# Matmuls whose result nobody reads, placed at six points of a two-block transformer kernel

## The chip, the cores and the metric

The kernel runs on one core of one Trainium2 chip. The metric is the device time of one execution in microseconds (us). Engines are named as the profile names them: PE is TensorE (PEld its weight loads), DVE is VectorE, ACT is ScalarE, POOL is GpSimd, SP is SyncE, which issues most transfers. [...]

## The reference, cut to what matters

512 tokens of width 1024 go through two blocks, all in float32. The first block has a layer of gated linear attention and a layer of dilated attention over three groups, whose outputs are weighted by a softmax over the groups' log-sum-exps. The second block has a layer of latent and grouped attention over 512 tokens and 256 context tokens, a mixture of 32 experts (each token goes to 2), a layer of neighbourhood attention, and a second mixture. Norms stand between layers.

```
def first_block(...):
    for i in range(DEPTH):                  # 0: gla_mixer, 1: dilated_mixer
        h = rmsnorm(x, norm_w[i])
        ...
        branch = jnp.concatenate([mix, mem_o], axis=-1) * jax.nn.silu(gate)
        x = x + branch @ w_out[i]
    return rmsnorm(x, final_norm_w)

def dilated_mixer(h, w_in):
    ...
    wts = jax.nn.softmax(jnp.stack(lses, axis=0), axis=0)
    o = jnp.einsum('gbth,gbthd->bthd', wts, jnp.stack(outs, axis=0).astype(jnp.float32))

def second_block(...):
    for l in range(DEPTH):                  # 0: mixer_ab, 1: mixer_na
        h_l = modulate(x_lat, norm_mix[l], sh1, sc1)
        ...
        x_lat = x_lat + g1 * o_l
        h_l = modulate(x_lat, norm_ffn[l], sh2, sc2)
        y = hier_moe(tokens, moe_w_rg[l], ..., moe_w_gate[l], moe_w_up[l], moe_w_down[l])
        x_lat = x_lat + g2 * y...

def hier_moe(h, ...):                       # for each block of 128 tokens of one expert e:
    return (jax.nn.silu(xb @ w_gate[e]) * (xb @ w_up[e])) @ w_down[e]
```

## The kernel before, in words

Nearly all products are three fp32r products in place of one f32 product (`mm3`, L259 to L261): both factors are cut into a high and a low part, and high x high, high x low and low x high are added up in PSUM. Weights are loaded by SP in chunks (`pump`, L182) into slots called `wraw`; ACT writes the high part `whi` (L208), DVE the low part `wlo` (L211). A slot takes the next chunk once its low part is cut. `K.ready` is the queue of cut chunks.

Each stage is written as generators that yield costs, and `weave` runs them against one another, so the program's text order is interleaved by these costs. A scheduler then sets the order of instructions on every engine from its own model; each engine works through its row in that order.

The six places that matter here:

- **The norms between layers** (`norm_T`, L367). Four rows of 128 tokens, `K.tok` (`xres` in the profile), are scaled by ACT and DVE into `y` (L377, L379); then for k = 0..7 four 128x128 transposes (L386) fill one PSUM tile `ps_t`, and ACT and DVE write its high and low part (`dhh`, `dhl` ahead of the dilated layer, L390 and L391; through `nt`, L395, elsewhere). Ahead of the dilated layer and the ab layer this follows the last output projection, whose products go through L259 to L261 and are added to `xres` at L826.
- **The sums of w_ada** run beside the dilated layer: SP loads w_ada, DVE adds scaled rows into `acc` (L1393, L1395), and a product with a vector of ones (L1400) adds up the partitions. They hold DVE when a transfer is late.
- **The dilated layer's last softmax** (`Dil.joint` for t = 2). PE transposes the statistics `stT` (L1327), ACT and DVE work out the weights `jw`, PE transposes these (L1345), ACT copies them to `c6` (`c` in the profile), DVE writes the low part (L1347), and six products with a selection matrix spread them (L1352); DVE multiplies the groups' outputs (L1353). `values` (L1307) and the projection of the next part (L259 to L261 on `b`) go on around it.
- **The two expert stages** (`experts`, L2070). A table is made on DVE and PE (`table`; its last products are L2019, its results `idx`, `blk`). `overflow` is a loop of `blk` rounds (L2045 loads the count, L2046 is the loop), none in this data. Then `xg[0]`, the first expert's 128 tokens, is gathered by an indirect DMA on POOL (L2181), transposed on PE (`transposed`, L2192) into `ps_x`, copied into high and low (`xth`, `xtl`, L139 and L140), and multiplied by the gate and up weights into `ps_h`.

## Time and profile before

| | |
|---|---|
| time, median of 3 runs | 3178.2 us (3174.72 to 3180.22) |
| the profiled execution | 3179.87 us, span 3178.1 us |
| mean granted clock of PE | 0.958 |
| busy in the span: DVE, ACT, POOL | 71%, 56%, 18% |
| the chain that ended last, by engine | PE 80%, DVE 8%, ACT 4%, DMA 3%, issue 2% |
| instructions of PE | 17454 matmuls, 17454 weight loads |

Times in the profile are counted from the start of the span. A row of a timeline gives start, duration, engine, line, operation and tiles, the count, and in brackets how long the engine was idle before it and what ended that. Products of PE overlap, so the distance from one start to the next is the price of one, not its duration. A step of the chain has the part of the duration that lies on the chain. An f32 product appears as two records.

### The profile page before, as it was taken

To read this page: it belongs to the slowest core of one execution; us is meant where nothing else is said; L and a number is where in the kernel's file an instruction comes from. 1 tells how busy PE (TensorE), PEld (TensorE's weight loads), DVE (VectorE), ACT (ScalarE), POOL (GpSimd) and SP (SyncE) were. 2 spreads that over 40 slices of the span, in tenths; PEclk is the share of its full clock that TensorE was granted. 3 is DMA by queue.
4 is the path that set the end of the run, shared out by engine and by line. 5 is a ranking of instruction groups with operands and counts; after the bars stand their busy time and mean duration, and the time that the engine had idled before them with its cause. 6 is when DMAs were issued, how large, how long until landed. Compare 5 with 4: busy or idle time off the path is not lost.

```text
span 3178.1 us, 46855 instructions
## 1 busy us (share of the span) xinstructions
PE 2932.0 (92%) x17454; PEld 2455.8 (77%) x17454; DVE 2270.2 (71%) x3743; ACT 1793.7 (56%) x2971; POOL 567.2 (18%) x869
## 2 busy tenths in 40 slices
PE   7989899999889889996999999969998789999997
PEld 6858688888779777786888888858886778888885
DVE  4776656765555566657998899875445678988888
ACT  4543534343352466533887788854334368878885
POOL 2110143523232211032111111020001211111110
PEclk9989999999889899996999999989999889999998
DMA  6334333433431200034999999954334389999996
GB/s 209 126 113 139 140 125 115 148 132 133 153 122 29 76 28 1 1 116 148 362 374 374 344 360 367 365 171 141 100 100 142 140 292 370 351 331 347 353 366 203
DMA packets 146090, 636.32 MB, mean 200 GB/s; under 512 B 30787, under 2 KB 37283, under 8 KB 86850
## 3 DMA queue, kind: packets, MB, share of 16 engines
q1 hardware_dynamic: 104034, 568.56, 49.3%
q0 software_dynamic: 29664, 50.29, 5.0%
q10 hardware_dynamic: 12160, 14.43, 1.9%
q8 instruction: 139, 2.28, 0.3%
q14 instruction: 93, 0.76, 0.1%
HBM read 615.13 MB, written 48.58 MB: 209 GB/s over the span
## 4 chain that ended last, share of the span: by engine, by line
PE 80%; DVE 8%; ACT 4%; DMA 3%; issue 2%; POOL 1%; ACTq 0%; DVEq 0%; SPq 0%; POOLq 0%
PE ps_p L259 10%; PE ps_p L261 9%; PE ps_p L260 9%; PE ps_h L260 8%; PE ps_h L259 7%; PE ps_h L261 7%; PE ps_y L260 4%; PE ps_y L261 4%; PE ps_y L259 4%; PE ps_x L2192 2%; PE ps_o L574 2%; PE ps_t L562 2%; DVE wlo L211 2%; PE ps_o L470 1%; PE ps_t L490 1%
## 5 line engine op out<-in xcount | busy, mean ns | idle before, releaser
L211 DVE TENSOR_TENSOR wlo<-wraw,whi 128x1024 fp32r<-128x1024 f32 (+1 forms) x936 | 1104.7, 1221 | 243.4 <-ACT whi L208 238.9
L208 ACT ACTIVATE whi<-wraw 128x1024 fp32r<-128x1024 f32 (+1 forms) x938 | 936.2, 1050 | 185.8 <-PE ps_p L260 53.8
L260 PE MATMUL ps_h<-wlo,xth 128*128 128x512 f32 x1024 | 415.6, 406 | 1.3 <-DVE wlo L211 1.1
L259 PE MATMUL ps_h<-whi,xth 128*128 128x512 f32 x1024 | 409.1, 399 | 2.9 <-ACT xth L139 2.9
L261 PE MATMUL ps_h<-whi,xtl 128*128 128x512 f32 x1024 | 404.9, 395 | 0.0
L259 PE MATMUL ps_p<-whi,dhh 128*128 128x256 f32 (+3 forms) x828 | 248.6, 301 | 9.6 <-ACT qa L1540 5.7
L260 PE MATMUL ps_p<-wlo,dhh 128*128 128x256 f32 (+3 forms) x828 | 240.4, 291 | 0.0
L261 PE MATMUL ps_p<-whi,dhl 128*128 128x256 f32 (+3 forms) x828 | 239.7, 291 | 0.0
L259 PEld LDWEIGHTS ps_h<-whi,xth 128*128 128x128 f32 x1024 | 193.9, 189 | 47.9 <-ACT xth L139 4.0
L260 PEld LDWEIGHTS ps_h<-wlo,xth 128*128 128x128 f32 x1024 | 193.9, 189 | 47.7 <-DVE wlo L211 7.4
L261 PEld LDWEIGHTS ps_h<-whi,xtl 128*128 128x128 f32 x1024 | 193.5, 189 | 40.0
L259 PE MATMUL ps_y<-whi,hth 128*128 128x512 f32 x512 | 204.8, 400 | 5.8 <-DVE xg L2124 2.9
L1395 DVE SCALAR_TENSOR_TENSOR acc<-wraw,cs,acc 128x512 f32<-128x512 f32 x280 | 203.1, 758 | 9.2 <-DMA wraw<-in_w_ada_dram 7.5
L260 PE MATMUL ps_y<-wlo,hth 128*128 128x512 f32 x512 | 202.5, 395 | 0.2
L261 PE MATMUL ps_y<-whi,htl 128*128 128x512 f32 x512 | 201.9, 394 | 0.0
L2181 POOL DMA_INDIRECT xg<-hbuf,idx x64 | 85.3, 1333 | 547.2 <-PE ps_x L2192 494.5
L259 PEld LDWEIGHTS ps_p<-whi,dhh 128*128 128x128 f32 x828 | 157.7, 191 | 24.7 <-ACT qa L1540 5.9
L260 PEld LDWEIGHTS ps_p<-wlo,dhh 128*128 128x128 f32 x828 | 158.0, 191 | 1.3
L261 PEld LDWEIGHTS ps_p<-whi,dhl 128*128 128x128 f32 x828 | 157.7, 191 | 1.3
L2258 POOL DMA_INDIRECT ybuf<-y,idx x62 | 66.1, 1067 | 465.4 <-ACT y L2254 451.4
L139 ACT ACTIVATE xth<-ps_x 128x512 fp32r<-128x512 f32 x128 | 75.4, 589 | 76.7 <-PE ps_h L260 40.9
L259 PEld LDWEIGHTS ps_y<-whi,hth 128*128 128x128 f32 x512 | 96.3, 188 | 27.7 <-ACT whi L208 3.3
(788 smaller groups left out, 6766.1 us busy)
## 6 DMA issues: line engine op xcount, KB each, us to landing
wraw<-in_moe_w_gate_dram SPq DMA_DIRECT2D x128, 1024.0 KB
wraw<-in_moe_w_up_dram SPq DMA_DIRECT2D x128, 1024.0 KB
wraw<-in_moe_w_down_dram SPq DMA_DIRECT2D x128, 1024.0 KB
wraw<-in_w_ada_dram SPq DMA_DIRECT2D x48, 1024.0 KB
wraw<-in_db_w_dram SPq DMA_DIRECT2D x27, 1024.0 KB
wraw<-in_w_out_dram SPq DMA_DIRECT2D x8, 1024.0 KB
wraw<-in_na_qk_dram SPq DMA_DIRECT2D x8, 1024.0 KB
ntab<-in_na_tab_dram SPq DMA_DIRECT2D x16, 384.0 KB
```

What stands on the lines that cost most here:

```text
L139: nc.scalar.activation(hi, src, AF.Copy)
L208: self.nc.scalar.activation(h, x, AF.Copy)
L211: (self.cut_eng or self.nc.vector).tensor_tensor(l, x, h.bitcast(F32), op=OP.subtract)
L259: mm(out, ah, bh, start=first, stop=False)
L260: mm(out, ah, bl, start=False, stop=False)
L261: mm(out, al, bh, start=False, stop=last)
L562: nc.tensor.transpose(ps[:, b:b + 128], u.P[:, u.at[h, i], cols[m]:cols[m] + 128], K.ident)
L574: nc.tensor.matmul(po[64 * h:64 * h + 64, c:c + m], u.V(kt, h), pts[n][:, o_ + h * m:o_ + (h + 1) * m], start=(a == 0), stop=(a == last), ...
L1395: nc.vector.scalar_tensor_tensor(acc[s], x, w, acc[s], op0=OP.mult, op1=OP.add)
L2181: self.K.nc.gpsimd.indirect_dma_start(out=xg, out_offset=None, in_=self.hbuf, in_offset=bass.IndirectOffsetOnAxis(ap=gi, axis=0), bounds_c ...
L2192: nc.tensor.transpose(px[:, j * 128:(j + 1) * 128], xv[:, j, :], K.ident)
L2258: self.K.nc.gpsimd.indirect_dma_start(out=self.ybuf, out_offset=bass.IndirectOffsetOnAxis(ap=si, axis=0), in_=y, in_offset=None, bounds_ch ...
```

## The change

A helper `busy` issues n matmuls into a PSUM tile that is written again, from the start, by what follows; nobody reads what they write. It is called at these places:

- `norm_T` with `alone=True`, at three norms (ahead of the dilated, the ab and the neighbourhood layer): 7 f32 products, 128x128 by 128x512, ahead of the first four transposes, and 1 ahead of the four of each k = 1..7.
- `Dil.joint` at t = 2: 7 f32 products on `stT` (68 partitions, 512 columns) behind the transposes of `stT`, and 3 fp32r products (6 partitions, 512 columns) behind the copy of `c6`.
- `experts`: 24 fp32r products, 128x128 by 128x512, on the high part of the first cut weights, in the text behind the gathers and ahead of `transposed(xg[0])`. Both mixtures have it.

```diff
--- before.py
+++ after.py
@@ -260,6 +260,12 @@
         mm(out, ah, bl, start=False, stop=False)
         mm(out, al, bh, start=False, stop=last)
 
+    def busy(self, ps, a, b, n):
+        for _ in range(n):
+            self.nc.tensor.matmul(ps[:, :b.shape[-1]], a, b, start=True, stop=True)
+
     def fm(self, nc_, blocks, xh, xl, nt, evac, tag="p", kt=8):
 
         hi, lo = self.take()
@@ -364,7 +370,7 @@
         self.nc.vector.tensor_copy(t, ps[:, :n])
         return t
 
-    def norm_T(self, pool, rows, rstd, hi, lo, sc, sh=None, tag="t", dst=None, src=lambda x: x):
+    def norm_T(self, pool, rows, rstd, hi, lo, sc, sh=None, tag="t", dst=None, src=lambda x: x, alone=False):
 
 
         nc = self.nc
@@ -382,6 +388,8 @@
         yield 0, 1500
         for k in range(8):
             ps = self.ps(tag)
+            if alone:
+                self.busy(ps, self.ident, rows[0][:, 0:512], 1 if k else 7)
             for i, y in enumerate(ys):
                 nc.tensor.transpose(ps[:, i * 128:(i + 1) * 128], y[:, k * 128:(k + 1) * 128], self.ident)
             h, l = (dst(x[:, k, :]) if dst else x[:, k, :w] for x in (hi, lo))
@@ -802,7 +810,7 @@
             rs = K.rsqrt(r.sum(range(4)), 4, 1.0 / D)
             yield 0, 2500
             yield from K.norm_T(st, K.tok, [rs[:, i:i + 1] for i in range(4)], K.dhh, K.dhl, nw,
-                                dst=phases, src=phase_order)
+                                dst=phases, src=phase_order, alone=True)
         weave(norms(), out_steps(K, range(4), tokens(bh, bl), r.add))
     K.close(gC)
     K.close(gA)
@@ -1129,7 +1137,7 @@
             rs = K.rsqrt(u, 4, 1.0 / D, 0.0)
             yield 0, 2500
             if K.stop != "b1":
-                yield from K.norm_T(st, K.tok, [rs[:, i:i + 1] for i in range(4)], hh, hl, sc[0], sh[0])
+                yield from K.norm_T(st, K.tok, [rs[:, i:i + 1] for i in range(4)], hh, hl, sc[0], sh[0], alone=True)
             rs = K.rsqrt(s1, 4, 1.0 / D)
             for t in range(4):
                 nc.vector.scalar_tensor_tensor(K.tok[t], K.tok[t], rs[:, t:t + 1], fw, op0=OP.mult, op1=OP.mult)
@@ -1325,6 +1333,8 @@
         pt = K.ps("t")
         for j in range(4):
             nc.tensor.transpose(pt[:, j * 128:j * 128 + 68], self.stT[0:68, j * 128:(j + 1) * 128], K.ident[:68, :68])
+        if t == 2:
+            K.busy(K.ps("S"), self.stT[0:68, 0:128], self.stT[0:68, :], 7)
         s = wk.tile([128, 4, 3, 4], F32, name="js")
         nc.scalar.activation(s, pt.rearrange("p (t g c) -> p t g c", t=4, g=4)[:, :, 0:3, 0:4], AF.Copy)
         m = wk.tile([128, 4, 2], F32, name="jm")
@@ -1344,6 +1354,8 @@
         for j in range(4):
             nc.tensor.transpose(pw[:6, j * 128:(j + 1) * 128], w[:, j].rearrange("p g c -> p (g c)"), K.ident)
         nc.scalar.activation(self.c6[0:6], pw[:6, :], AF.Copy)
+        if t == 2:
+            K.busy(K.ps("S"), self.sel[0:6, 0, :], self.c6[0:6, :], 3)
         ve.tensor_tensor(self.c6[32:38], pw[:6, :], self.c6[0:6].bitcast(F32), op=OP.subtract)
         yield 256, 1500
         for h in range(2):
@@ -2079,6 +2091,7 @@
 
             for e in range(NE - TAIL, NE):
                 self.scatter(xg[2], self.idx[:, 1, e:e + 1])
+            K.busy(K.ps("x"), K.ready[0][0][:, 0:128], K.ready[0][0][:, 0:512], 24)
             b = self.transposed(xg[0])
             for f in later:
                 f()
@@ -2300,7 +2313,7 @@
 
     def lat():
         rs = K.rsqrt(ss[:, 0:4], 4, 1.0 / D)
-        yield from K.norm_T(p, K.tok, [rs[:, i:i + 1] for i in range(4)], hh, hl, sc[0], sh[0],
+        yield from K.norm_T(p, K.tok, [rs[:, i:i + 1] for i in range(4)], hh, hl, sc[0], sh[0], alone=True,
                             dst=lambda x: x[:, 64:576].rearrange("p (c r) -> p r c", r=8),
                             src=lambda t: t.rearrange("p (r c) -> p r c", c=64))
         nc.scalar.activation(hh[:, :, 0:64], hh[:, :, 512:576].bitcast(F32), AF.Copy)
```

In the changed kernel lines are numbered 6 to 13 higher, so L2046 becomes L2058, L2192 becomes L2205, L386 becomes L394, L1400 becomes L1412; the products of `busy` are L267.

PE's order at the start of the first expert stage, from the last rows of the overflow loop on, before:

```order
L2046 REGISTER_ALU
L2046 COMPARE_AND_BRANCH
L2046 UNCONDITIONAL_BRANCH
L2192 MATMUL ps_x<-ident,xg_14992 128x128 x8
L259 MATMUL ps_h<-whi,xth 128x512
L260 MATMUL ps_h<-wlo,xth 128x512
```

The same rows of PE now:

```order
L2058 REGISTER_ALU
L2058 COMPARE_AND_BRANCH
L2058 UNCONDITIONAL_BRANCH
L267 MATMUL ps_x<-whi 128x512 x24
L2205 MATMUL ps_x<-ident,xg_15032 128x128 x8
L259 MATMUL ps_h<-whi,xth 128x512
L260 MATMUL ps_h<-wlo,xth 128x512
```

The 24 products stand between the loop and the transposes; the second stage reads the same. POOL's order didn't move: there the gather of `xg[0]` stands ahead of the load of `blk` and of the loop's rows, before and now.

PE's order at the norm ahead of the dilated layer, from the last products of the out-projection on, before (`acc` is the sum of w_ada, `y` a scaled row of tokens):

```order
L259 MATMUL ps_p<-whi,bh 128x256
L260 MATMUL ps_p<-wlo,bh 128x256
L261 MATMUL ps_p<-whi,bl 128x256
L1400 MATMUL ps_a<-acc_82,ones_75 32x512
L1400 MATMUL ps_a<-acc_83,ones_75 32x512
L386 MATMUL ps_t<-ident,y_2872 128x128
L386 MATMUL ps_t<-ident,y_2874 128x128
...
```

The same place of PE now, and after the dots the transposes of k = 4 and 5:

```order
L259 MATMUL ps_p<-whi,bh 128x256
L260 MATMUL ps_p<-wlo,bh 128x256
L261 MATMUL ps_p<-whi,bl 128x256
L267 MATMUL ps_t<-xres,ident 128x512 x8
L1412 MATMUL ps_a<-acc_82,ones_75 32x512
L1412 MATMUL ps_a<-acc_83,ones_75 32x512
L394 MATMUL ps_t<-ident,y_2872 128x128
...
L267 MATMUL ps_t<-xres,ident 128x512
L394 MATMUL ps_t<-ident,y_2872 128x128
L394 MATMUL ps_t<-ident,y_2874 128x128
L394 MATMUL ps_t<-ident,y_2876 128x128
L394 MATMUL ps_t<-ident,y_2878 128x128
```

Eight of the fourteen stand together behind the out-projection, two more among its products, and one ahead of the four transposes of each of k = 4 to 7. At the ab layer's norm it is one, nine and four; at the neighbourhood layer's norm seven, and one ahead of the transposes of each k from 1 to 7. DVE's order changes at the first norm too: of eight `dhl` in a row the last four have ada sums between them.

PE's order at the dilated layer's last softmax, before (`xres` is `stT` here, `c` is `c6`):

```order
L1327 MATMUL ps_t<-ident,xres 128x68 x4
L1307 MATMUL ps_o<-PT,dv 128x128 x4
L1400 MATMUL ps_a<-acc_82,ones_75 32x512
L1345 MATMUL ps_t<-ident,jw 6x128 x4
L1352 MATMUL ps_S<-c_3640,sel 128x512 x6
```

And now:

```order
L1335 MATMUL ps_t<-ident,xres 128x68 x4
L267 MATMUL ps_S<-xres 128x512
L1315 MATMUL ps_o<-PT,dv 128x128 x4
L267 MATMUL ps_S<-xres 128x512 x6
L1355 MATMUL ps_t<-ident,jw 6x128 x4
L1412 MATMUL ps_a<-acc_82,ones_75 32x512
L267 MATMUL ps_S<-c_3654,sel 128x512 x3
L1364 MATMUL ps_S<-c_3654,sel 128x512 x6
```

The seven products come ahead of the transposes of `jw`, six of them behind `values`' products; the ada product has moved behind those transposes, and the three short ones stand ahead of the spreading.

## Rows read from the trace of the kernel before

**Rows 1.** The page, part 1: busy us (share of the span) xinstructions.

```profile
PE 2932.0 (92%) x17454; PEld 2455.8 (77%) x17454; DVE 2270.2 (71%) x3743; ACT 1793.7 (56%) x2971; POOL 567.2 (18%) x869
```

**Rows 2.** The chain at the first expert stage: start us, us, what.

```profile
1488.11 0.22 POOLq L2045
1488.33 6.66 DMA xg<-hbuf,idx
...
1498.71 0.79 PE ps_h L259
1499.50 0.43 PE ps_h L260
...
1502.33 0.23 PE ps_h L260
```

**Rows 3.** Timeline of PE: transposes at the stage's start and later in it.

```profile
1496.05 1.97 PE L2192 MATMUL ps_x<-ident,xg 128*128 128x128 f32 x8 [8.96 <-issue]
...
1511.39 1.05 PE L2192 MATMUL ps_x<-ident,xg 128*128 128x128 f32 x8
```

**Rows 4.** Windows: us, busy PE PEld DVE ACT POOL, PEclk, DMA share, GB/s.

```profile
1450.00:1488.00 38.00, 22.30 (x131) 21.57 (x130) 29.73 (x104) 15.24 (x33) 1.55 (x3) 0.51 0.46 180
1488.00:1496.00 8.00, 0.00 (x0) 0.00 (x0) 4.30 (x10) 0.26 (x1) 1.76 (x1) 0.50 0.45 143
...
1520.00:2060.00 540.00, 539.80 (x2500) 443.07 (x2499) 480.96 (x472) 440.47 (x532) 67.32 (x57) 1.00 0.98 365
...
873.00:887.50 14.50, 11.28 (x47) 10.01 (x47) 6.61 (x9) 3.26 (x6) 9.03 (x9) 0.50 0.63 229
```

**Rows 5.** Timelines of DVE and ACT at the start of the first expert stage.

```profile
1487.24 0.24 DVE L1919 SCALAR_TENSOR_TENSOR idx<-ps_h,z 128x86 int32<-128x86 f32 x1
...
1495.95 0.21 DVE L2120 CAST ti<-idx 128x1 f32<-128x1 int32 x2 [3.69 <-DMA xg<-hbuf,idx]
...
1495.74 1.28 ACT L139 ACT_TABLE_LOAD   x1 [10.33 <-DMA xg<-hbuf,idx]
```

**Rows 6.** The chain at the second expert stage.

```profile
2545.59 6.97 DMA xg<-hbuf,idx
...
2554.14 1.98 PE ps_x L2192 x8
```

**Rows 7.** Timeline of PE: another restart with dense products, 2101 to 2107 us.

```profile
2101.06 0.79 PE L2158 MATMUL ps_h<-xtl,oh 128*128 128x512 f32 x1 [4.77 <-DVE xtl L140]
...
2106.30 0.39 PE L2157 MATMUL ps_h<-xth,oh 128*128 128x512 f32 x1
```

**Rows 8.** Waits of SP's DMA queue, 1520 to 2060 us: total, times, longest.

```profile
SPq L182 <- DVE wlo L211: 469.3, 177, 4.5
```

**Rows 9.** Timeline of PE: one f32 product of 512 columns at either clock level.

```profile
863.04 1.91 PE L1400 MATMUL ps_a<-acc,ones 128*32 128x512 f32 x2 [3.81 <-DVE acc L1395]
...
890.97 1.04 PE L1400 MATMUL ps_a<-acc,ones 128*32 128x512 f32 x2
```

**Rows 10.** Timeline of PE: its pauses at the three norms.

```profile
330.47 2.56 PE L1400 MATMUL ps_a<-acc,ones 128*32 128x512 f32 x4 [5.39 <-DVE ringdtfloat L339]
333.94 3.67 PE L386 MATMUL ps_t<-ident,y 128*128 128x128 f32 x16 [0.91 <-ACT y L379]
...
942.31 4.54 PE L386 MATMUL ps_t<-ident,y 128*128 128x128 f32 x24 [7.67 <-ACT y L379]
...
2114.43 5.99 PE L386 MATMUL ps_t<-ident,y 128*128 128x128 f32 x28 [5.64 <-ACT y L379]
...
2129.07 0.58 PE L259 MATMUL ps_p<-whi,nhh 128*128 128x256 f32 x1 [6.51 <-ACT nhh L2306]
```

**Rows 11.** The chain behind the first norm.

```profile
346.81 6.89 DMA wraw<-in_w_ada_dram
```

**Rows 12.** Timeline of PE at the dilated layer's last softmax.

```profile
869.06 1.22 PE L1352 MATMUL ps_S<-c,sel 128*128 128x512 f32 x2 [3.16 <-DVE c L1347]
...
881.61 0.58 PE L259 MATMUL ps_p<-whi,b 128*128 128x256 f32 x1 [1.65 <-ACT b L139]
```

## The prediction

> **What bounds the kernel now.** I read the page's first part, then the chain of waits and the timelines at each of the six places that the diff touches, then a table of windows for the granted clock. TensorE (PE) is busy for 92% of the span [rows 1], so work put on it is free only where PE truly waits. The largest of the six are the starts of the two expert stages. There the chain runs through the indirect gather of the first expert's tokens, 6.66 us, then eight transposes of these tokens, and only then comes the first product at 1498.71 us [rows 2]. [...]

> [...] DVE's cast of `ti` (L2120) reads only `idx`, which DVE itself wrote at 1487.24 us, and yet it stood behind the gather until 1495.95 us; ACT's table load stood behind it until 1495.74 us [rows 5]. In POOL's order the gather of `xg[0]` stands ahead of the overflow loop, though the code calls it behind (in the chain `POOLq L2045`, the load of the loop's count, and the transfer stand side by side [rows 2]). So it is the exit of that loop that holds every engine until the gather has landed, not the transposes' own wait. In the second layer PE, DVE and the gather stand in the same way: 6.97 us of transfer, transposes at 2554.14 us [rows 6].

> **The 24 products of an expert stage.** The order has them on PE behind the loop's last row and ahead of the transposes. They read weights that are cut by then, so nothing but the loop's exit holds them, and that exit comes with the gather landed. They therefore don't run beside the gather. They run in front of transposes whose data is already there, straight on the path.

> [...] In between, take the nearest restart of dense 512-column products after a pause: from 2101.06 us to the first one of 0.23 us pace at 2106.30 us, 5.2 us [rows 7]. That is 12 products at 0.43 and leaves 12 at 0.23: 5.2 + 2.8 = 8.0 us.

> They give something back, since what follows finds the clock up. Eight transposes cost 1.97 us at the start and 1.05 us later in the stage [rows 3]: 0.9 us. The eight products from 1498.71 to 1502.33 us took 3.62 us and would take 8 x 0.23 = 1.84 us: 1.8 us. Net 8.0 - 0.9 - 1.8 = 5.3 us for a layer, 10.6 us for two. Ends: 5.5 - 2.7 = 2.8 us and, if the clock doesn't rise, 10.3 us, so 5.6 to 20.6 us for two.

> [...]

> Does a late start pass to the end? From 1520 to 2060 us PE is busy for 539.8 of 540 us at clock 1.00 [rows 4]; the weight loads wait 469.3 us for slots that DVE's cuts free [rows 8]. The loads are ahead of PE: I pass the whole delay on.

> **The three norms.** Fourteen f32 products each. The trace has one such product of 512 columns as two records: 1.04 us at the high level, 1.91 us at the low one [rows 9]. Ahead of the dilated layer eight stand together behind the out-projection (two more stand among its products, four later): 8 x 1.0 = 8 us into a gap of 5.39 us and one of 0.91 us behind the ada products [rows 10], so the transposes start some 1.5 us late, then run faster (sixteen took 3.67 us there). The last four products stand among the second sixteen transposes: up to 4 us more. But the chain from there doesn't go over PE: it goes over DVE's `dhl` and its ada sums to a transfer of 6.89 us, whose slot these sums set free, and to more ada sums behind it [rows 11]. The order puts ada sums between the last `dhl`, so the slot comes free about as before. I take +0.5 us, ends -1 and +4.

> Ahead of the ab layer nine products (9 us) meet a gap of 7.67 us: about 1.3 us late, given back by faster transposes and by the first products behind them. Ahead of the neighbourhood layer seven (7 us) meet 5.64 us, seven more stand among transposes that ran at the low level; the end there is ACT's, PE waits 6.51 us for it, and a start 1 us later would move it [rows 10]. If instead the clock stays up until that layer's projection, about 20 products that were at 0.21 us save 0.09 us each, 1.9 us. Both: 0 us, ends -2 and +3.

> **The dilated layer's last softmax.** Seven f32 products stand among `values`' last ones and ahead of the transposes of `jw`, three fp32r ones behind the ada product. From 857.2 us, with 2.0 us of `values` among them, 5.2 us at the low level (some 3 products) and 4 us at the high one, they end near 868.5 us. The transposes of `jw` ran some 4 us earlier than that, but what they feed waited anyway: PE stood 3.16 us for `c` until 869.06 us, DVE being behind an ada transfer [rows 12]. So the weighting starts about 1.4 us later. Against this, of the 47 products at clock 0.50 until 887.5 us [rows 4], 0.21 us apart, the 27 behind the last wait at 881.61 us [rows 12] would save 0.09 us each, 2.5 us. Net -1 us, ends -2.5 and +3.6 (no rise of the clock: the transposes of `jw` later still).

> **Sum.** 10.6 + 0.5 + 0 - 1 = 10.1 us. The profiled execution took 3179.87 us, 1.8 us around its span of 3178.1; 3179.87 + 10.1 = 3190.0 us. It was 1.7 us above the median of 3178.2 us, so against that median I predict 3188.5 us.

> **Rivals.**
> - A: the products run beside the gather. Then PE keeps its clock for nothing: 2 x 2.7 us back at the expert stages, 2.5 us at the softmax, 1 + 2 us at the norms: 10.9 us faster, 3167 us. For it: PE's 8.96 us of idle time is there, and would hold 8.0 us of products. Against it: DVE's cast and ACT's table load show the exit of the loop as what is waited for [rows 5]. [...] 7%.
> - B: the stage takes the delay up. The transfers' share is 0.98 in 1520 to 2060 us [rows 4]; were they the bound, 5 us at the start would be made good by loads that go on meanwhile: 3178 us. Against it: the loads' own waits for slots. 12%.
> - C: the products don't raise the clock, as PE's work ahead of the gather, 22.3 us of 38, left it at 0.51 [rows 4]: 20.6 us, 3197 us. Against it: dense 512-column products raised it at both restarts. 5%.
> - D: the products of norms and softmax are late in full: 4 + 3 + 3.6 us in place of -0.5, so 3199 us. For it: each group is longer than its gap. Against it: transfers and ACT end these stretches. 8%.
> - My forecast, slower by 5 to 16 us: 68%.

> **Range and chances.** About 0.2%, 6.4 us, is what a measurement of this kernel can tell from no change. Faster is most of A: 0.06. Within 0.2% are B, the rest of A, and the forecast where the softmax and norms give back 4 us more than I took (an eighth of it): 0.21. Slower: 0.73. The range goes from 3177 us, which takes in B, to 3197 us, which takes in C, and leaves out A and D.

> **What would show it.** In the profile after, L267 as a group `ps_x<-whi` x48, about 8 us in each layer, beginning when the gather has landed (near 1496 us), with the transposes behind it at about 1.05 us instead of 1.97. If L267 begins within a microsecond of the gather's issue, or if `ps_h`'s first product comes before 1500 us plus what earlier stages shifted, I am wrong and A holds. If the expert stage's length from its first product to its last has shrunk by about what its start lost, B holds. A granted clock of 0.50 through L267 speaks for C. How much later or earlier the products behind each norm and behind the softmax begin, against before and against what already came earlier, tells those terms.

## The result, and the profile after

The changed kernel takes 3199.5 us (median of 4 runs, 3192.4 to 3204.7) against 3179.1 us before: ratio 1.0066, 95% interval 1.0053 to 1.0079. Measured again with more runs it is 3196.4 us, ratio 1.0058 (1.0046 to 1.0071). The change makes the kernel 15 to 25 us slower; forecast were 10 us, and the median lies beyond the range's end of 3197 us. The profiled execution, 3192.39 us, was the fastest of the four; that this one comes near the forecast is luck, as the part on the prediction shows.

The page of the changed kernel, the parts that answer to [rows 1] and the granted clock in 40 slices:

```profile
PE 2974.2 (93%) x17603; PEld 2474.9 (78%) x17603; DVE 2272.0 (71%) x3743; ACT 1793.4 (56%) x2971; POOL 567.5 (18%) x869
...
PEclk9989999999999999997999999979999899999998
```

PE has 149 more records and is busy 42 us longer. The time of the other engines hasn't moved. The granted clock reads 9 in 35 of the 40 slices, before in 31 (mean 0.962 against 0.958), and the kernel is slower: here the clock is not the measure.

The chain at the first expert stage after, as [rows 2] before:

```profile
1485.34 6.43 DMA xg<-hbuf,idx
1491.77 1.07 issue
1492.84 7.65 PE ps_x L267 x24
```

The timeline of PE at the same place and at the second stage, as [rows 3]:

```profile
1492.84 7.63 PE L267 MATMUL ps_x<-whi 128*128 128x512 f32 x24 [8.74 <-issue]
1500.53 1.16 PE L2205 MATMUL ps_x<-ident,xg 128*128 128x128 f32 x8
1502.38 0.50 PE L259 MATMUL ps_h<-whi,xth 128*128 128x512 f32 x1 [0.69 <-ACT xth L139]
...
2562.21 7.14 PE L267 MATMUL ps_x<-whi 128*128 128x512 f32 x24 [10.08 <-DVE ti L2133]
2569.41 1.16 PE L2205 MATMUL ps_x<-ident,xg 128*128 128x128 f32 x8
```

The 24 products begin 1.07 us after the gather has landed, not beside it: PE sits idle for 8.74 us, where before it were 8.96 [rows 3]. They take 7.6 and 7.1 us, at a granted clock of 0.50 from 1492.84 to 1495.00 us and of 1.00 from 1497.00 us on. The transposes then take 1.16 instead of 1.97 us, and the products behind them start at 1.00 (1502.38 to 1504.00 us), where before they started at 0.51 (1498.70 to 1502.06 us). In the prediction and below, low stands for a granted clock of 0.50 or for the prices measured at it, high for one of 1.00 or its prices.

Where the time went is read best by matching every instruction with its counterpart before and taking the median shift over some 40 us on either side of a place; the difference is what that place costs. Us, by that reckoning, in the traces (norm 1 is ahead of the dilated layer, 2 of the ab layer, 3 of the neighbourhood layer):

| trace | norm 1 | softmax | norm 2 | experts 1 | norm 3 | experts 2 | at the end |
|---|---|---|---|---|---|---|---|
| the change | 0.0 | -2.9 | +0.3 | +5.4 | +4.8 | +5.2 | +13.0 |
| e1_again, the same kernel | +1.0 | +5.3 | +0.3 | +5.5 | +1.8 | +4.8 | +19.2 |
| e2_moe_only | | | | +6.6 | | +4.7 | +9.5 |
| e3_no_moe | +0.7 | +5.4 | +0.3 | | +2.7 | | +9.0 |
| e4_joint_only | | +5.3 | | | | | +4.5 |
| e4b_joint_128 | | -2.9 | | | | | +2.6 |
| e5_norm3_only | | | | | +3.0 | | +2.8 |
| e9_norm3_first | | | | | -2.9 | | -1.6 |
| e10_best | | -1.3 | | | -2.9 | | +3.0 |

Cells are left empty where a kernel has nothing at the place. Stretches that no kernel changes scatter by some 2 us, near 2450 us by up to 5 us, so the last column holds more than the others. The second expert stage stands close behind that place: over 20 us on either side its three figures are +5.2, +5.9 and +5.7 us.

### The profile page after: what moved, and what is told of

It is laid out like the page before. It is cut to its first block, busy times and chain, and to the rows that moved or that the text cites. A ratio compares the mean times of both kernels' runs of the same rounds, so it can differ in the third digit from the quotient of the medians.

```text
span 3190.6 us, 47154 instructions
## 1 busy us (share of the span) xinstructions
PE 2974.2 (93%) x17603; PEld 2474.9 (78%) x17603; DVE 2272.0 (71%) x3743; ACT 1793.4 (56%) x2971; POOL 567.5 (18%) x869
## 4 chain that ended last, share of the span: by engine, by line
PE 81%; DVE 9%; ACT 4%; DMA 3%; issue 2%; POOL 1%; ACTq 0%; DVEq 0%; SPq 0%; POOLq 0%
PE ps_p L259 10%; PE ps_p L261 9%; PE ps_p L260 9%; PE ps_h L260 7%; PE ps_h L259 7%; PE ps_h L261 7%; PE ps_y L260 4%; PE ps_y L261 4%; PE ps_y L259 4%; PE ps_x L2205 2%; PE ps_o L582 2%; PE ps_t L570 2%; DVE wlo L211 2%; PE ps_o L478 1%; PE ps_t L498 1%
## 5 line engine op out<-in xcount | busy, mean ns | idle before, releaser
L259 PE MATMUL ps_p<-whi,dhh 128*128 128x256 f32 (+3 forms) x828 | 247.6, 299 | 10.1 <-ACT qa L1552 5.9
```

The lines of the kernel that those rows point to most:

```text
L259: mm(out, ah, bh, start=first, stop=False)
```

## Experiments

Parts of the change were run alone, each timed beside the kernel before.

**The changed kernel again** (no edit).

> The changed kernel once more, timed against before on one chip, and with a second profile. My theory: the cost is two terms, 5.3 us at the start of each expert stage and about 4 us at the norm ahead of the neighbourhood layer, less 2.5 us at the softmax: +12 to +13 us, as in its first profile, and the further 8 us of the median are scatter of the other stretches. Rival: the median of +20 us stands again, so a term of some 8 us is missing from the first profile, and the second profile shows it at one place.

Measured +18.6 us on the medians. The rival holds: the missing term is at one place, the softmax. At its place the timeline of PE in the first trace of the change:

```profile
856.40 0.47 PE L1335 MATMUL ps_t<-ident,xres 68*128 68x68 f32 x4 [1.69 <-DVE xres L1324]
856.70 1.07 PE L267 MATMUL ps_S<-xres 68*128 68x512 f32 x2
...
858.50 5.32 PE L267 MATMUL ps_S<-xres 68*128 68x512 f32 x12
863.66 0.60 PE L1355 MATMUL ps_t<-ident,jw 128*6 128x128 f32 x4
```

and in the second:

```profile
858.83 0.71 PE L1335 MATMUL ps_t<-ident,xres 68*128 68x68 f32 x4 [1.70 <-DVE xres L1324]
859.34 2.01 PE L267 MATMUL ps_S<-xres 68*128 68x512 f32 x2
...
862.85 10.45 PE L267 MATMUL ps_S<-xres 68*128 68x512 f32 x12
873.09 1.06 PE L1355 MATMUL ps_t<-ident,jw 128*6 128x128 f32 x4
```

Behind the same pause of 1.7 us the granted clock is 1.00 in one execution (857 to 864 us) and 0.50 in the other, and where it is 0.50 the seven products do not raise it: the windows of the second trace have 0.50 throughout, with PE busy without a gap for 15 us.

```profile
859.00:865.00 6.00, 6.00 (x17) 3.83 (x18) 5.89 (x9) 3.91 (x6) 0.00 (x0) 0.50 0.72 207
865.00:874.00 9.00, 9.00 (x14) 3.22 (x12) 0.79 (x5) 0.22 (x1) 0.41 (x1) 0.50 0.53 213
```

Who waits for it is DVE, which writes the low part of `c`. Its timeline before, where that instruction stood behind an ada transfer, and then in the second trace, where DVE is idle for 8.70 us ahead of it:

```profile
867.02 0.49 DVE L1393 TENSOR_SCALAR acc<-wraw,cs 128x512 f32<-128x512 f32 x1 [1.29 <-DMA wraw<-in_w_ada_dram]
...
868.33 0.68 DVE L1347 TENSOR_TENSOR c<-ps_t,c 6x512 fp32r<-6x512 f32 x1
```

```profile
874.80 0.68 DVE L1359 TENSOR_TENSOR c<-ps_t,c 6x512 fp32r<-6x512 f32 x1 [8.70 <-ACT c L1356]
```

It starts 6.5 us later than before; 2.1 us of that come from earlier stages.

**The expert stages alone** (`alone=True` goes at all three norms).

```
-                                dst=phases, src=phase_order, alone=True)
+                                dst=phases, src=phase_order)
...
-            K.busy(K.ps("S"), self.stT[0:68, 0:128], self.stT[0:68, :], 7)
...
-            K.busy(K.ps("S"), self.sel[0:6, 0, :], self.c6[0:6, :], 3)
```

> Only the 24 products at both expert stages. My theory: they run behind the loop's exit, 7.7 us each time, and what follows gets 2.5 us back: +10.5 us (9 to 12). Rival, the products are cheap and the norms cost: under +4 us. Rival, everything else of the +20 us is in the expert stages too: +18 us or more.

3188.6 us against 3177.7: +10.8 us, ratio 1.0047 (1.0029 to 1.0064); its trace has +6.6 and +4.7 us at the two stages. The first theory holds. The interval is wide, since two of seven executions took 12 us more.

**All but the expert stages.**

```
-            K.busy(K.ps("x"), K.ready[0][0][:, 0:128], K.ready[0][0][:, 0:512], 24)
```

> The change without the 24 products, so norms and softmax alone. My theory: norm ahead of the neighbourhood layer +4, softmax -2.5, the other two norms 0: +1 to +2 us. Rival, the norms carry the missing 8 us: +8 to +10 us.

+5.3 us, ratio 1.0016 (1.0004 to 1.0027), between the two expectations. Its trace has the softmax at the low clock (10.45 us for the last six of the seven products), +5.4 us.

**The softmax alone**, and then with all 128 rows of `stT` (the order on each engine is the same):

```
-            K.busy(K.ps("S"), self.stT[0:68, 0:128], self.stT[0:68, :], 7)
+            K.busy(K.ps("S"), self.stT[:, 0:128], self.stT, 7)
```

> Only the ten products at the dilated layer's last softmax. The traces so far show two outcomes: clock high at 857 us, the seven f32 products take 6.4 us and the stretch gains 2.5 us; or clock low there, all seven stay low, take 12.4 us, and the stretch loses 5.5 us. My theory: mostly the second, +3 to +5 us on the median, with a scatter of some 8 us between the executions. Rival: the products raise the clock often enough, -2.5 to 0 us.

> As the softmax's products alone, but the seven f32 products read all 128 partitions of stT instead of 68 (the lower 60 rows are zeros). Same order on every engine. My theory: what keeps the clock low in them is that they use only a part of the array's rows; with 128 rows the clock rises within some 5 us as at other restarts, the seven take 8 to 9 us instead of 12.4, and the median is 0 to -2 us. Rival: the rows don't matter (most of stT is zeros, or f32 products do too little), the products stay low for 12.4 us and the time is that of the 68 rows.

68 rows: +6.1 us on the medians, ratio 1.0018 (1.0007 to 1.0029), the clock low in the trace (10.45 us for the last six products), +5.3 us: the theory, a little larger. 128 rows: +2.6 us, ratio 1.0005 (0.9996 to 1.0014), which is not told apart from before nor from 68 rows; its trace found the clock high (1.07 us for the first product, 5.32 for the six others) and so doesn't test the rise. The trace of the last version below does: there the first product costs what it costs at the low clock, and the timeline of PE and two windows read

```profile
860.59 0.59 PE L1335 MATMUL ps_t<-ident,xres 68*128 68x68 f32 x4 [1.70 <-DVE xres L1324]
860.97 2.02 PE L267 MATMUL ps_S<-xres 128*128 128x512 f32 x2
...
864.34 5.32 PE L267 MATMUL ps_S<-xres 128*128 128x512 f32 x12
```

```profile
859.00:864.00 5.00, 3.42 (x12) 2.38 (x13) 4.90 (x8) 3.77 (x6) 1.01 (x2) 0.68 0.34 97
864.00:870.00 6.00, 6.00 (x20) 2.78 (x18) 3.38 (x9) 2.10 (x3) 0.04 (x1) 0.98 0.98 355
```

The first product costs 2.02 us, the six others 5.32 instead of 10.45, and the windows read 0.68 and then 0.98: with 128 rows the clock rose, in the one trace that found it low. In all three traces that found it low, 68 rows left it there, at 10.45 us for the six. PE's order and the columns are the same and the added rows are zeros, so in these four traces the rise came with the added rows, though they hold only zeros. With 128 rows that is a single trace.

**Norm 3 alone, and its first seven products alone.**

```
-            if alone:
-                self.busy(ps, self.ident, rows[0][:, 0:512], 1 if k else 7)
+            if alone and not k:
+                self.busy(ps, self.ident, rows[0][:, 0:512], 7)
```

> Only the 14 products of the norm ahead of the neighbourhood layer. My theory: the products of k = 1..7 let the order put the context's multiplication (yc, which waits for a transfer) ahead of the last low parts nhl on DVE; the projection then starts some 5 us later, of which 4 us stay: +4 us, and DVE's yc with a wait of over 3 us for its transfer ahead of nhl. Rival, the products' own time on PE delays the norm: PE's last transposes late by 5 us or more, and no such wait on DVE.

> Of the norm ahead of the neighbourhood layer only the seven products ahead of the first transposes, none at k = 1..7. In DVE's order yc then stands behind all of nhl, as before the change. My theory: the cost of this norm was DVE's wait for yc, so it goes: 0 us (-1 to +1.5). Rival: the seven at the front are what costs, as they are 7 us in a pause of 5.6: +4 us as with all fourteen.

All fourteen: +5.3 us, ratio 1.0017 (1.0009 to 1.0026), and the wait for `yc` stands in that trace, 5.15 us. The first seven: ratio 0.9991 (0.9982 to 1.0000), -2.2 us on the medians, -2.9 us in the trace, better than the theory's 0: the transposes behind them stand 0.12 us apart (26 in 3.06 us), where [rows 10] has 28 in 5.99, 0.21 us apart, at a granted clock of 0.50 (2114.43 to 2119.30 us). Why fourteen cost, DVE's timeline in the changed kernel shows:

```profile
2128.75 1.10 DVE L140 TENSOR_TENSOR nhl<-nt,nhh 128x512 fp32r<-128x512 f32 x1 [1.21 <-ACT nhh L139]
2134.53 1.23 DVE L2188 TENSOR_TENSOR yc<-yc,gc 128x1024 f32<-128x1024 f32 x1 [4.67 <-DMA yc<-ybuf]
2135.67 1.07 DVE L140 TENSOR_TENSOR nhl<-nt,nhh 128x512 fp32r<-128x512 f32 x1
```

`yc` belongs to the context and waits for a transfer; the low part `nhl` behind it has nothing to wait for. Before, `yc` stood behind all of `nhl` (at 2130.13 us, idle 0.55 us). With the products at k = 1..7 the scheduler puts `yc` between, and without them it doesn't; that its model expects later transposes is the likely reason, not shown. The chain in the changed kernel goes over these products as well, since POOL issues the transfer of `yc` behind PE's transposes:

```profile
2128.69 0.97 POOL L2145 DMA_DIRECT2D yc<-ybuf  x1 [2.83 <-PE ps_t L394]
```

PE's timeline, first for the changed kernel, then with seven products, answers to the last of [rows 10]:

```profile
2139.36 0.58 PE L259 MATMUL ps_p<-whi,nhh 128*128 128x256 f32 x1 [9.76 <-ACT nhh L2319]
```

```profile
2126.88 0.58 PE L259 MATMUL ps_p<-whi,nhh 128*128 128x256 f32 x1 [6.66 <-ACT nhh L2314]
```

**Norms 1 and 2**, together, apart, and norm 1 with its first seven products alone (the edit as above).

> Only the products of the norms ahead of the dilated and the ab layer. The traces of the change had the dilated layer's start 0 to +1 us later than before, where kernels without these products had it 1.3 to 2.6 us earlier; the ab layer's start was level. My theory: +1 to +2 us. Rival from the sums, since norms and softmax together cost no more than the softmax or the last norm alone: they gain some 5 us.

> Only the 14 products of the norm ahead of the dilated layer. Theory: of the two norms this one costs, since it alone also changes the order of DVE and ACT behind it (ada sums among the last dhl, the first attention units in another order): +5 to +8 us, with executions on two levels some 8 us apart. Rival: level, and the cost is at the ab layer's norm.

> Only the 14 products of the norm ahead of the ab layer; DVE's and ACT's order are those of before. Theory: 0 us (-1 to +1). Rival: nine f32 products, 9 us in a pause of 7.7 us, and four more among the transposes: +5 to +8 us.

Together +7.3 us, ratio 1.0021 (1.0009 to 1.0033); norm 1 alone ratio 1.0029 (1.0019 to 1.0040), norm 2 alone 1.0012 (1.0000 to 1.0025), with +2.0 us on the medians and +0.3 us in every trace. The first and the third of these expectations were too low, the second has about the size. Two further traces:

> The two norms again, one more trace: the first showed +0.4 us, where the median says +7. Theory: a slower execution shows the missing time at one place, between the dilated layer's norm and its first attention units (300 to 400 us). Rival: spread over many places.

> The two norms once more, for a further trace, with the same theory and rival as the look before.

These two executions took 3182.6 and 3179.9 us, less than the 3185.7 us that the timed ones have as their median, and show +2.4 and +1.2 us at norm 1.

> Of the norm ahead of the dilated layer only the seven products ahead of the first transposes; none at k = 4 to 7. ACT's order behind the norm is that of all fourteen, so are the first attention units' products on PE. If the four late products cost: 0 to +2 us. If the order behind the norm (or the seven at the front) costs: +7 to +9 us as with all fourteen.

> All fourteen products of the norm ahead of the dilated layer once more, timed beside the run above and with a second trace. If the +9 us stands: +6 to +10 us again; its trace, if of a slower execution, shows the place. If it was scatter: +1 to +3 us, which is what the stretch from 300 to 400 us shows in the traces.

Fourteen products again: ratio 1.0017 (1.0008 to 1.0026). The first seven: 1.0005 (0.9995 to 1.0015), level on the medians. So the cost goes with the seven products of k = 1 to 7. More than the four late ones leaves with them: three stood at the front, and DVE's order changes too, as its timeline with fourteen and then with seven shows. The runs don't tell these three apart.

```profile
341.17 2.72 DVE L399 SCALAR_TENSOR_TENSOR dhl<-ps_t,nw,dhh 128x512 fp32r<-128x512 f32 x4
...
344.29 0.75 DVE L399 SCALAR_TENSOR_TENSOR dhl<-ps_t,nw,dhh 128x512 fp32r<-128x512 f32 x1
344.95 0.74 DVE L1403 SCALAR_TENSOR_TENSOR acc<-wraw,cs,acc 128x512 f32<-128x512 f32 x1
```

```profile
339.81 5.35 DVE L399 SCALAR_TENSOR_TENSOR dhl<-ps_t,nw,dhh 128x512 fp32r<-128x512 f32 x8
```

The trace with fourteen is of an execution above its median, 3185.5 us, and still doesn't show the place that was looked for: -0.1 us at norm 1, +5.7 us at the end. The timeline of PE with fourteen:

```profile
336.86 2.13 PE L394 MATMUL ps_t<-ident,y 128*128 128x128 f32 x16 [1.11 <-ACT y L385]
341.97 1.12 PE L267 MATMUL ps_t<-xres,ident 128*128 128x512 f32 x2 [2.98 <-DVE dhl L399]
342.93 0.60 PE L394 MATMUL ps_t<-ident,y 128*128 128x128 f32 x4
343.37 1.02 PE L267 MATMUL ps_t<-xres,ident 128*128 128x512 f32 x2
```

and with the first seven:

```profile
336.38 3.35 PE L394 MATMUL ps_t<-ident,y 128*128 128x128 f32 x16 [3.27 <-ACT y L385]
340.60 2.63 PE L394 MATMUL ps_t<-ident,y 128*128 128x128 f32 x16 [0.87 <-DVE dhl L399]
```

There are four tiles `ps_t`, and the product of k = 4 writes the tile that the transposes of k = 4 will write. So it waits for DVE's `dhl` to free it, 2.98 us, as these transposes do. It can't run in the wait; it runs when the wait is over, ahead of what was waited for.

**Products beside the gather.** First in the kernel with the loop, ahead of it (six f32 products):

```
+            ix = self.idx.rearrange("p k b -> p (k b)").bitcast(F32)
+            K.busy(K.ps("x")[:2 * NB], ix, K.ready[0][0][:, 0:512].bitcast(F32), 6)
             nov = nc.values_load(self.blk[0:1, 0:1], min_val=0, max_val=NB - NE)
```

> In place of the 24 products behind the overflow loop: six f32 products (86 by 512 columns, stationary the table idx, so that they start when it is written) ahead of the loop, beside the gather. My theory: they run from 1487.5 us on and end near 1496 us, the gather is not held, transposes and first products behind them run at the high clock: 2.0 to 2.7 us back at each stage, -4 to -5.4 us. Rival: the loop's entry waits for PE, and the stage starts as late or later, 0 to +2 us; or 86 columns don't raise the clock, 0 us.

The rival's mechanism holds, at more than its price: ratio 1.0019 (1.0007 to 1.0031), +6.1 us on the medians, +3.6 and +2.7 us at the two stages. The timeline of PE:

```profile
1482.48 7.70 PE L267 MATMUL ps_x<-whi,idx 128*86 128x512 f32 x12 [0.45 <-DVE idx L1927]
1493.91 1.97 PE L2202 MATMUL ps_x<-ident,xg 128*128 128x128 f32 x8 [3.72 <-SPq L2056]
...
2553.59 1.98 PE L2202 MATMUL ps_x<-ident,xg 128*128 128x128 f32 x8 [4.52 <-DVE ti L2130]
```

The products ran beside the gather, which landed at 1489.61 us. But the engines leave the loop together, although it has no round (ACT's next instruction starts at 1493.70 us, DVE's at 1493.82, PE's at 1493.91): from PE's arrival at 1490.18 us it takes 3.7 us, at the second stage 4.5. The stage starts later, and the transposes cost 1.97 us, as before the change, where the granted clock was 0.50 (1496.00 to 1498.70 us): by this price the clock is low behind the wait. Then both kernels without the loop:

```
-            m.overflow()
```

> Before the change, without the overflow loop (it leaves out the rounds for experts with more than 128 tokens, of which this data has none). Theory one, the loop's passage holds the engines some 3.6 us after the last of them arrives, and the gather alone would let PE go about 1 us earlier: 1 to 2 us less at each stage, -2 to -4 us. Theory two, of the prediction, the exit only waits for the gather: 0 to -1 us at each stage.

> The same without the loop, with six f32 products on idx (86 rows of result, 512 columns) on PE ahead of the transposes, so that they run beside the gather. My theory: nothing holds them now, they take 7 to 7.7 us from the time idx is written, end as the gather lands, and PE starts the transposes at the high clock: 2.0 to 2.7 us less at each stage than without the loop alone, -4 to -5.4 us against that kernel. Rival: the gather lands earlier than they end, and the stage gains 0 to 1 us.

Without the loop: ratio 1.0009 (0.9999 to 1.0019), no gain in time, while its trace has -0.9 us at the second stage and +0.4 at the first. The transposes do start earlier against the gather, 0.05 us after it has landed in place of 1.06, as theory one has it, but the 2 to 4 us don't come of it. With the products beside the gather: ratio 0.9987 (0.9978 to 0.9996) against the kernel before, 8.2 us less on the medians than without the loop alone, where 4 to 5.4 were expected; by the shifts in the traces the stages gain 1.1 and 2.6 us against that kernel (2.7 and 2.4 over 20 us on either side). The timeline of PE:

```profile
1486.06 7.24 PE L267 MATMUL ps_x<-whi,idx 128*86 128x512 f32 x12 [0.45 <-DVE idx L1927]
1493.63 1.13 PE L2202 MATMUL ps_x<-ident,xg 128*128 128x128 f32 x8 [0.34 <-DMA xg<-hbuf,idx]
1495.45 0.50 PE L259 MATMUL ps_h<-whi,xth 128*128 128x512 f32 x1 [0.69 <-ACT xth L139]
```

The products fill the wait to within 0.34 us, the transposes cost 1.13 us, and the first real product takes 0.50 us in place of 0.79 [rows 2], with the next ones 0.23 us apart (1495.79, 1496.02 us). That is rival A, with other products than the change's; the run before it shows that with these same products the loop keeps the kernel from it. This kernel leaves out the overflow rounds and is no replacement.

**What is left of the change** (norm 3's first seven, the softmax with 128 rows):

> What the runs leave of the change: seven products ahead of the first transposes of the norm ahead of the neighbourhood layer, the softmax's seven with 128 rows and its three short ones; nothing at the expert stages and at the other norms. My theory: -3 us from the norm, -2.5 to +1 from the softmax, -2 to -5 us in all. Rival: the softmax's products stay at the low clock in many executions and take it back, 0 to +2 us; a trace with clock 0.50 at the transposes of stT shows whether 128 rows raise it.

Ratio 0.9997 (0.9988 to 1.0006): not told apart from before. The best version for all data is norm 3's first seven alone, 0.9991, with an interval that ends at 1.0000.

## Why the prediction was wrong

**The step that failed** is the softmax: "5.2 us at the low level (some 3 products) and 4 us at the high one", net -1 us with ends of -2.5 and +3.6. It took from [rows 7], products of 128 rows with a granted clock of 0.50 from 2101.06 to 2105.90 us and of 1.00 from 2106.30 us on, that any dense products raise the clock. Those of 68 rows didn't: some 12 us of them stayed at 0.50, and the place cost +5.3 us in three of four traces; -2.9 us only in the trace that has 1.00 there. Against +10.1 us forecast, this is some 6 us of the missing 10. Its own end for no rise, +3.6 us, was too small as well: seven products at 1.91 us [rows 9] end at 872.6 us in place of 868.5, and with the 1.4 us that is some 5.5 us. In the second trace of the change the missing 9.1 us are found: 6.3 at the softmax, 1.8 at norm 3, the rest at the other norms and in unchanged stretches. The first trace has +13.0 us, near the forecast, because its clock happened to be at 1.00 at the softmax while norm 3 cost 4.8 us.

**Norm 3** was put at 0 us together with norm 2 and cost +1.8 to +4.8 in the traces, +5.3 alone. I weighed the products on PE and counted nothing for DVE, whose order showed `yc` ahead of `nhl`. The seven ahead of the transposes, which I feared would be late, gain 2.9 us.

**Norm 1** was put at +0.5 us with ends of -1 and +4; alone it cost +5.4 and +9.2 us by the two ratios. That the four late products wait for a tile, and then stand ahead of their transposes, is shown; that the transfer behind them would take this up was only argued, and holds in part. In the traces with all fourteen the projection behind the norm starts some 3 us later, against kernels without these products, and by 400 us about 2 us of that are left. The times show more, and where the rest arises stays open. The parts also don't add up: alone they come to some 30 us on the medians, together to 19 or 20. Norms and softmax together cost less than norm 1 or the softmax alone would suggest; what they share is open.

**The expert stages** came as worked out: 5.3 us each were forecast, 5.4 and 5.2 measured in the first trace, 5.5 and 4.8 in the second. The price (8.0 us, measured 7.1 to 8.5) and the 2.7 us given back were right to within 1 us. The ends for the products of a stage, 5.5 and 10.3 us, are 24 times the 0.23 and the 0.43 us of [rows 2], where the granted clock was 1.00 (1502.33 to 1504.00 us) and 0.51 (1498.70 to 1502.06 us). The whole delay passed on to the end, against rival B: the shift of 2.4 us behind the first stage is still 2.4 us at 2050 us. The reason holds too: in all 17 traces in which nothing stands on PE ahead of the loop, DVE's first instruction behind it starts 0.96 us after the gather has landed at the first stage and 1.33 to 1.36 us at the second, however long DVE itself has stood at the loop (3.4 to 4.3 us at the first). What the reason left out is the loop's own passage, which shows where PE comes to it late (e7_moe_moved).

Rival A was right in its mechanism and had no place to act. Rival C (no rise of the clock) came true at the softmax (0.50 from 859 to 874 us in the second trace), where the forecast had it only as an end. Rival D, products late in full, has 3199 us and is nearest to the result; it got 8%. It is right at the softmax, while at norm 3 the cost came over DVE. Two sums were off besides: against the median of 3178.2 us the forecast is 3188.3, not 3188.5 us, and C's own 20.6 us give 3198.8, not 3197 us, so the range did not take C in.

## What to carry to other kernels

At the expert stages work that keeps the clock up paid only where it ran while its engine waited: behind the gather it cost 5.4 and 5.2 us, beside it, with no loop ahead, it gained 1.1 and 2.6 us against the same kernel without it. Look at which buffer it writes (one product waited 2.98 us for its tile), which loop or branch stands ahead of it, and whether a wait that it should fill holds it too. Measure from a low start whether it raises the clock at all, since a high start hides that it does nothing; here products on 68 rows didn't raise it in three traces, and products on 128 rows did in one. An instruction added to one engine can move the order on the others, as at norms 1 and 3; compare those rows, and look for a wait on a transfer that has come ahead of something ready (4.67 us for `yc`).
